# Split first loads, zero matmuls ahead of the data, and other numbers in the instruction order of a two-layer decoder trunk

## The chip, the core and the metric

The kernel runs on one core of a Trainium2 chip. The metric is the device time of one execution in microseconds (us), the median of several runs. Five engines work side by side, each through its own list of instructions in a fixed order: TensorE (PE in the profile, with its weight loads shown apart as PEld), VectorE (DVE), ScalarE (ACT), GpSimd (POOL) and SyncE (SP, which here only issues DMA transfers). An instruction whose input is not there holds up everything behind it on its engine.

## The reference

Two layers, each with one RMS norm, one wide projection and three parallel mixers; 512 tokens, 1024 features, float32 throughout. Cut to what matters:

```python
def reference(x, norm_g, w_in, ..., w_o):
    for l in range(DEPTH):                                   # DEPTH = 2
        h = rms_norm(x, norm_g[l])
        p = h @ w_in[l]                                      # 1024 -> 8776 columns
        (cb, cc, cx, cgate, q, k, v, agate, iq, ik, iw, pu, pgate, mgate) = split_columns(p)
        y_a = short_conv_mixer(cb, cc, cx, cgate, conv_w[l], w_out_conv[l])
        y_b = sparse_attention_mixer(q, k, v, agate, iq, ik, iw, ...)   # indexer, top 128 keys, softmax, 8 heads
        y_c = pool_mixer(pu, pgate, pool_w[l], pool_scale[l], w_out_pool[l])
        g = jax.nn.sigmoid(mgate.reshape(B, S, N_BRANCHES, D))
        merged = g[:, :, 0] * y_a + g[:, :, 1] * y_b + g[:, :, 2] * y_c
        x = x + merged @ w_o[l]
    return x
```

## The kernel before, in words

Everything is held transposed: features on the 128 partitions, the 512 tokens along the row. The input x is eight tiles of 128x512 (`xT[k]`), the weights are a stream of 180 chunks of 128x1024 (`wst`), 90 for each layer. Every float32 operand is split into a high part in the matmul format and the rest (`split`: ScalarE writes `hi`, VectorE subtracts and writes `lo`), and each product is three matmuls, hi by hi, hi by lo and lo by hi (`mm3`). A projection (`project`) is thus 8 slices of 3 matmuls of 128x512, 24 in all, that add up in one PSUM tile `pj`; there are four such tiles. A chunk of weights is loaded into one of two `raw` tiles and split into one of three pairs `whi` and `wlo` (`prep`); chunks are prepared three ahead (`LOOK`).

At the start the vectors `vt` (norm gains) and the x tiles are loaded, all from SyncE's queue, each x tile split with its gain (`load_x`: `xhi`, `xlo`, and a square that GpSimd adds into `ss`). The first three chunks are loaded between them, the first in four pieces, the next two in two pieces each. `wavefront` then runs three projections at once, slice by slice over k.

After that a layer runs the indexer (`select`: PE products in `sc` tiles, then 16 rounds of max and match_replace on VectorE for each of three query blocks), the pooling mixer, queries and keys (`normed`), values, the two attention passes (`attention`: scores in `sc`, transposes in `pt`, values in `pv`), the convolution mixer, three merges and the output projection.

The order written in the code is not the order that runs. The class `Order` reads all instructions with what they depend on, plays them on a model of the engines (`play`) with a duration for each (`cost`) and a delay from one engine to another (`lat`; `TO_PE` is the delay up to a matmul), and fixes the order that it finds on each engine. An engine takes, of the instructions that are ready, the one with the smallest priority; on PE the priority is the place in the code. `arrange` repeats this with new priorities (`PASSES`) and keeps the shortest. The delay from one matmul to the next that adds to the same tile is 0.003 there, so that next matmul is not yet ready at the moment PE is free, and another tile's matmul goes first.

Of the kernel before, what the change touches and what calls it, by code (L numbers as in the profile page):

```python
# [5 lines left out]
F32 = mybir.dt.float32  # L6
F32R = mybir.dt.float32r
AF = mybir.ActivationFunctionType
ALU = mybir.AluOpType
PSUM = bass.MemoryType.PSUM  # L10

LAG = 3
PASSES = 4
P = 128
S = 512
D = 1024
KT = D // P
# [12 lines left out]
class Order:  # L30
# [4 lines left out]


    LAT = {"PE": 0.2, "DVE": 0.13, "Activation": 0.14, "Pool": 0.1, "SP": 0.13}
    TO_PE = {"PE": 0.003, "DVE": 0.255, "Activation": 0.27, "Pool": 0.2, "SP": 0.27}

    def lat(self, a, b):  # L40
        return self.TO_PE[a] if b == "PE" else self.LAT[a]
# [66 lines left out]
    def cost(self, inst, kind):  # L108

        def size(a):  # L110
            n = 1
            for _, k in a.bass_ap.ap[1:]:
                n *= k
            return n

        aps = [a for a in inst.ins if hasattr(a, "bass_ap")]
        out = inst.outs[0]
        n = size(out)
        psum = any(a.bass_ap.tensor.name.split("_")[0] in ("pj", "sc", "pt", "pv") for a in aps)
        wide = [a for a in aps if size(a) > 1]  # L120
        extra = len(aps) > len(wide)
        engine = str(inst.engine).split(".")[-1]
        if kind == "InstMatmult":
            f32 = str(aps[0].dtype).endswith("float32")
            c = (0.0004167 * n + 0.003) * ((4 if n > 128 else 2) if f32 else 1)
            return c, 0.0
        if kind == "InstDMACopy":
            b = n * out.bass_ap.ap[0][1] * 4
            return (0.65 if aps[0].bass_ap.tensor.name in self.slot else 0.48), b / 360e3
        if engine == "Activation":  # L130
            return 0.093 - 0.042 * psum + 0.000833 * n + 0.093 * extra, 0.0
        if engine == "Pool":
            return (0.1 if kind == "InstMemset" else 0.1 + 0.0022 * n), 0.0
        if kind in ("InstMax", "InstMatchReplace"):
            return 0.069 + 0.00104 * max(size(a) for a in aps), 0.0
        fast = kind == "InstTensorScalarPtr" and len(wide) == 1 and not psum
        return 0.069 + 0.00104 * n * (0.5 if fast else 1) + 0.061 * extra, 0.0

# [164 lines left out]
def trunk(ctx, tc, xT, wst, vecs, cst, outT):  # L303
    nc = tc.nc
    order = Order(tc)
# [3 lines left out]
    wp = pool("wp", 3)  # L309
# [7 lines left out]
    dve, act, pe, gp = nc.vector, nc.scalar, nc.tensor, nc.gpsimd  # L317
# [11 lines left out]
    def nm(s):  # L329
        uid[0] += 1  # L330
        return f"{s}_{uid[0]}"

    def W(dt=F32, n=S):
        return wk.tile([P, n], dt, tag="w", name=nm("w"))
# [4 lines left out]
    def big(dt=F32R):  # L339
        return bp.tile([P, 4, S], dt, tag="b", name=nm("b"))  # L340
# [7 lines left out]
    def pt():  # L348
        return pp.tile([P, 4, P], F32, tag="pt", name=nm("pt"), bufs=1)
# [1 line left out]
    def pv():  # L351
        return pp.tile([P, S], F32, tag="pv", name=nm("pv"), bufs=1)

    def load(dst, src):
        nc.sync.dma_start(dst, src)  # L355


    wq = {}
# [3 lines left out]
    def prep(i):  # L362
        l, c = divmod(i, NCHUNK)
        raw = wp.tile([P, 1024], F32, tag="raw", name=nm("raw"), bufs=2)
        hi = wp.tile([P, 1024], F32R, tag="whi", name=nm("whi"), bufs=3)
        lo = wp.tile([P, 1024], F32R, tag="wlo", name=nm("wlo"), bufs=3)
        n = 1024 // (4 if i == 0 else 2 if i < 3 else 1)
        for j in range(0, 1024, n):
            p = slice(j, j + n)
            load(raw[:, p], wst[l, c, :, p])  # L370
            act.activation(hi[:, p], raw[:, p], AF.Copy)  # L371
            dve.tensor_tensor(out=lo[:, p], in0=raw[:, p], in1=hi[:, p].bitcast(F32), op=ALU.subtract)  # L372
        wq[i] = (hi, lo)

    def take():
# [11 lines left out]
    def mm(ps, lhs, rhs, start, stop):  # L387
        pe.matmul(ps, lhs, rhs, start=start, stop=stop)  # L388
# [9 lines left out]
    def split(hi, lo, src, scale=None):  # L398
        if scale is None:
            act.activation(hi, src, AF.Copy)  # L400
            dve.tensor_tensor(out=lo, in0=src, in1=hi.bitcast(F32), op=ALU.subtract)  # L401
        else:
            act.activation(hi, src, AF.Copy, scale=scale)  # L403
            dve.scalar_tensor_tensor(lo, src, scale, hi.bitcast(F32), op0=ALU.mult, op1=ALU.subtract)
# [34 lines left out]
    xs = dp.tile([KT, P, S], F32, name="xs")  # L439


    load(vt, vecs)
    for k in range(KT):
        if k in (0, 2, 4):
            prep(state["next"])
            state["next"] += 1
        if k % 4 == 0:
            xin = big(F32)
        load(xin[:, k % 4], xT[k])
        load_x(0, k, xin[:, k % 4])  # L450
    load(ct, cst)
    ob = cp.tile([P, 2, P], F32R, name="ob")
# [11 lines left out]
    def wavefront(n, src, head):  # L464

        ws = [take() for _ in range(n)]
        pss = [pj() for _ in range(n)]
        ks = [range(KT - 1), [KT - 1]]
        order = [(u, k) for k in range(KT) for u in range(n)] if head else [(u, k) for part in ks for u in range(n) for k in part]
        for u, k in order:  # L470
            c = slice(k * P, (k + 1) * P)
            mm3(pss[u], ws[u][0][:, c], ws[u][1][:, c], *src(k), k == 0, k == KT - 1)
        return pss
# [470 lines left out]
```

## Time and profile before

| | |
|---|---|
| median of 3 runs | 1079.21 us (1078.87 to 1079.73) |
| the profiled execution | 1078.84 us |
| its span, first to last instruction | 1077.1 us |
| PE busy | 1065.4 us, 4842 matmuls |
| DVE, ACT, POOL busy | 799.2, 465.5, 97.2 us |

The profile is of one execution. Its own time is 1.74 us above its span, and 0.37 us below the median of the three runs. Matmuls overlap their neighbours in the pipeline, so the busy time of PE doesn't tell how densely it works; the spacing of their starts does.

### The profile page before, as it was taken

The numbers are of one execution on the slowest core, as the hardware profiler recorded it, in microseconds if no ns is written. First come the engines' busy times: TensorE is split into PE (matmuls) and PEld (weight loads), VectorE is DVE, ScalarE is ACT, GpSimd is POOL, SyncE is SP. The second block draws the span as 40 slices with busy tenths as digits, with TensorE's granted clock in tenths as the row PEclk, the third lists the DMA queues.
The fourth block names the chain that finished last, engine by engine and source line by source line (L and its number), as shares of the span: only waits on it lengthen the run. The fifth ranks groups of instructions, "written<-read, shape, count | busy, mean of one in ns | idle before, by whom it ended". The sixth has DMA issues, their size and how long they took to land.

```text
span 1077.1 us, 13444 instructions
## 1 busy us (share of the span) xinstructions
PE 1065.4 (99%) x4842; PEld 878.4 (82%) x4842; DVE 799.2 (74%) x1389; ACT 465.5 (43%) x747; POOL 97.2 (9%) x76
## 2 busy tenths in 40 slices
PE   7999999999999999999999999999999999999998
PEld 6888888888888888888888888888888878888886
DVE  6889999997558865455559899999876598744442
ACT  6355233485233673233334542235852347623320
POOL 4000000000000011221210000000000001132210
PEclk9999999999999999999999999999999999999999
DMA  6542322452234522234535322225423245122352
GB/s 226 153 140 78 99 98 94 133 152 72 82 102 130 160 75 78 98 98 164 169 117 153 115 86 98 98 79 166 128 79 98 79 144 149 61 98 98 98 195 78
DMA packets 44402, 124.39 MB, mean 115 GB/s; under 512 B 6960, under 2 KB 7472, under 8 KB 44336
## 3 DMA queue, kind: packets, MB, share of 16 engines
q1 hardware_dynamic: 44336, 123.53, 36.4%
q8 instruction: 38, 0.62, 0.2%
q14 instruction: 28, 0.23, 0.1%
HBM read 101.49 MB, written 4.19 MB: 98 GB/s over the span
## 4 chain that ended last, share of the span: by engine, by line
PE 96%; DVE 1%; DMA 1%; issue 0%; ACT 0%; SPq 0%; DVEq 0%; ACTq 0%
PE pj L388 87%; PE sc L388 4%; PE pv L388 3%; PE pt L391 2%; DMA b<-in_x 0%; DVE wlo L372 0%; DMA k<-h 0%; DVE w L488 0%; SPq L355 0%; DVE h L401 0%; ACT whi L371 0%; DVE w L649 0%; ACT xhi L403 0%; DVE w L435 0%; DVE w L436 0%
## 5 line engine op out<-in xcount | busy, mean ns | idle before, releaser
L388 PE MATMUL pj<-xhi,whi 128*128 128x512 f32 x1040 | 373.1, 393 | 6.5 <-ACT whi L371 6.5
L388 PE MATMUL pj<-xlo,whi 128*128 128x512 f32 x1040 | 372.8, 393 | 0.0
L388 PE MATMUL pj<-xhi,wlo 128*128 128x512 f32 x1040 | 372.4, 393 | 0.0
L371 ACT ACTIVATE whi<-raw 128x1024 fp32r<-128x1024 f32 (+2 forms) x185 | 191.5, 1036 | 385.6 <-PE pj L388 358.9
L372 DVE TENSOR_TENSOR wlo<-raw,whi 128x1024 fp32r<-128x1024 f32 (+2 forms) x185 | 228.5, 1239 | 15.5 <-ACT whi L371 14.8
L388 PEld LDWEIGHTS pj<-xhi,whi 128*128 128x128 f32 x1040 | 195.0, 188 | 46.7 <-ACT whi L371 6.7
L388 PEld LDWEIGHTS pj<-xhi,wlo 128*128 128x128 f32 x1040 | 195.7, 188 | 39.4 <-DVE wlo L372 0.5
L388 PEld LDWEIGHTS pj<-xlo,whi 128*128 128x128 f32 x1040 | 195.5, 188 | 39.4
L388 PE MATMUL pj<-b,whi 128*128 128x512 f32 x640 | 210.7, 390 | 0.0
L385 DVE TENSOR_TENSOR w<-pj,ss 128x512 f32<-128x512 f32 x104 | 70.8, 684 | 93.3 <-PE pj L388 93.0
L388 PEld LDWEIGHTS pj<-b,whi 128*128 128x128 f32 x640 | 120.0, 188 | 24.2
L388 PE MATMUL pj<-b,wlo 128*128 128x512 f32 x320 | 118.2, 391 | 0.0
L610 POOL TENSOR_TENSOR b<-b,w 128x512 f32<-128x512 f32 x32 | 60.6, 1899 | 264.5 <-DVE w L608 264.4
L388 PEld LDWEIGHTS pj<-b,wlo 128*128 128x128 f32 x320 | 60.1, 188 | 12.3
L576 DVE MAX8 m<-score 128x8 f32<-128x256 f32 (+2 forms) x96 | 53.2, 557 | 1.7
L577 DVE MATCH_REPLACE8 score<-m,score 128x384 f32<-128x384 f32 (+2 forms) x96 | 52.0, 542 | 0.0
L742 DVE TENSOR_TENSOR pth<-pt,pth 128x128 fp32r<-128x128 f32 (+1 forms) x64 | 31.1, 486 | 18.7 <-PE pv L388 9.4
L819 DVE TENSOR_TENSOR w<-pj,w 128x512 f32<-128x512 f32 x16 | 11.0, 690 | 44.4 <-PE pj L388 42.8
L727 ACT ACTIVATE a<-a,mn 128x128 f32<-128x128 f32 (+1 forms) x64 | 35.6, 557 | 15.5 <-DVE mn L724 14.9
L665 POOL TENSOR_TENSOR w<-w,w 128x512 f32<-128x512 f32 x8 | 11.9, 1492 | 325.4 <-ACT w L664 325.4
L388 PE MATMUL pv<-pth,b 128*128 128x512 f32 (+3 forms) x128 | 39.9, 316 | 0.0
L741 ACT ACTIVATE pth<-pt 128x128 fp32r<-128x128 f32 (+1 forms) x64 | 27.6, 432 | 27.4 <-PE pt L391 20.1
(119 smaller groups left out, 999.7 us busy)
## 6 DMA issues: line engine op xcount, KB each, us to landing
raw<-in_w SPq DMA_DIRECT2D x177, 512.0 KB, 3.3
b<-h SPq DMA_DIRECT2D x128, 64.0 KB, 2.2
k<-h SPq DMA_DIRECT2D x64, 128.0 KB, 3.2
b<-in_x SPq DMA_DIRECT2D x8, 256.0 KB, 4.8
w<-in_x SPq DMA_DIRECT2D x8, 256.0 KB, 5.5
xs<-w SPq DMA_DIRECT2D x8, 256.0 KB, 2.3
w<-xs SPq DMA_DIRECT2D x8, 256.0 KB, 3.9
out_x<-w SPq DMA_DIRECT2D x8, 256.0 KB, 2.0
```

What stands on the lines that cost most here:

```text
L371: act.activation(hi[:, p], raw[:, p], AF.Copy)
L372: dve.tensor_tensor(out=lo[:, p], in0=raw[:, p], in1=hi[:, p].bitcast(F32), op=ALU.subtract)
L385: dve.tensor_tensor(out=out, in0=ps, in1=by, op=ALU.mult)
L388: pe.matmul(ps, lhs, rhs, start=start, stop=stop)
L391: pe.transpose(out, src, ident if n == P else ident[64:64 + n, 64:64 + n])
L576: dve.max(m8, score)
L577: dve.match_replace(score, m8, score, -3.0e38)
L610: gp.tensor_tensor(out=a, in0=a, in1=g, op=ALU.add)
L665: gp.tensor_tensor(out=s0, in0=s0, in1=s1, op=ALU.add)
L727: act.activation(pr[:, :w], pr[:, :w], AF.Exp, bias=mn, scale=-1.0, accum_out=zs)
L741: act.activation(dh, pst[:, :b + 1, :], AF.Copy)
L742: dve.tensor_tensor(out=dl, in0=pst[:, :b + 1, :], in1=dh.bitcast(F32), op=ALU.subtract)
```

## The change

Five edits. The first x tile is loaded from ScalarE's queue. The first three chunks of weights are loaded in pieces of one, one, two and four slices, each just after the x tile that its slices belong to, into two spare `b` tiles instead of `raw`, and the vectors come behind x's first tile. Six matmuls of a zeroed tile run on PE ahead of the first real one. The first wavefront takes slices 6 and 7 of a projection together. And `Order` has other numbers: no delay between two matmuls, a longer matmul, longer GpSimd operations and match_replace, and six passes instead of four.

```diff
@@ -10,7 +10,8 @@
 PSUM = bass.MemoryType.PSUM
 
 LAG = 3
-PASSES = 4
+PASSES = 6
+WARM = 6
 P = 128
 S = 512
 D = 1024
@@ -35,7 +36,7 @@
 
 
     LAT = {"PE": 0.2, "DVE": 0.13, "Activation": 0.14, "Pool": 0.1, "SP": 0.13}
-    TO_PE = {"PE": 0.003, "DVE": 0.255, "Activation": 0.27, "Pool": 0.2, "SP": 0.27}
+    TO_PE = {"PE": 0.0, "DVE": 0.255, "Activation": 0.27, "Pool": 0.2, "SP": 0.27}
 
     def lat(self, a, b):
         return self.TO_PE[a] if b == "PE" else self.LAT[a]
@@ -122,7 +123,7 @@
         engine = str(inst.engine).split(".")[-1]
         if kind == "InstMatmult":
             f32 = str(aps[0].dtype).endswith("float32")
-            c = (0.0004167 * n + 0.003) * ((4 if n > 128 else 2) if f32 else 1)
+            c = (0.000423 * n + 0.01) * ((4 if n > 128 else 2) if f32 else 1)
             return c, 0.0
         if kind == "InstDMACopy":
             b = n * out.bass_ap.ap[0][1] * 4
@@ -130,9 +131,10 @@
         if engine == "Activation":
             return 0.093 - 0.042 * psum + 0.000833 * n + 0.093 * extra, 0.0
         if engine == "Pool":
-            return (0.1 if kind == "InstMemset" else 0.1 + 0.0022 * n), 0.0
+            return (0.1 if kind == "InstMemset" else 0.1 + 0.003 * n), 0.0
         if kind in ("InstMax", "InstMatchReplace"):
-            return 0.069 + 0.00104 * max(size(a) for a in aps), 0.0
+            n = max(size(a) for a in aps)
+            return 0.069 + 0.00104 * n + 0.076 * (kind == "InstMatchReplace"), 0.0
         fast = kind == "InstTensorScalarPtr" and len(wide) == 1 and not psum
         return 0.069 + 0.00104 * n * (0.5 if fast else 1) + 0.061 * extra, 0.0
 
@@ -351,8 +353,8 @@
     def pv():
         return pp.tile([P, S], F32, tag="pv", name=nm("pv"), bufs=1)
 
-    def load(dst, src):
-        nc.sync.dma_start(dst, src)
+    def load(dst, src, queue=nc.sync):
+        queue.dma_start(dst, src)
 
 
     wq = {}
@@ -364,12 +366,8 @@
         raw = wp.tile([P, 1024], F32, tag="raw", name=nm("raw"), bufs=2)
         hi = wp.tile([P, 1024], F32R, tag="whi", name=nm("whi"), bufs=3)
         lo = wp.tile([P, 1024], F32R, tag="wlo", name=nm("wlo"), bufs=3)
-        n = 1024 // (4 if i == 0 else 2 if i < 3 else 1)
-        for j in range(0, 1024, n):
-            p = slice(j, j + n)
-            load(raw[:, p], wst[l, c, :, p])
-            act.activation(hi[:, p], raw[:, p], AF.Copy)
-            dve.tensor_tensor(out=lo[:, p], in0=raw[:, p], in1=hi[:, p].bitcast(F32), op=ALU.subtract)
+        load(raw, wst[l, c])
+        split(hi, lo, raw)
         wq[i] = (hi, lo)
 
     def take():
@@ -439,14 +437,32 @@
     xs = dp.tile([KT, P, S], F32, name="xs")
 
 
-    load(vt, vecs)
+
+    idle = W(F32R)
+    gp.memset(idle.bitcast(F32), 0.0)
+    warm = pt()
+    for n in range(WARM):
+        mm(warm.rearrange("p a b -> p (a b)"), idle[:, :P], idle, n == 0, n == WARM - 1)
+    FIRST = 3
+    raws = [big(F32).rearrange("p (a b) s -> p a (b s)", a=2) for _ in range(2)]
+    firsts = []
+    for i in range(FIRST):
+        hi = wp.tile([P, 1024], F32R, tag="whi", name=nm("whi"), bufs=3)
+        lo = wp.tile([P, 1024], F32R, tag="wlo", name=nm("wlo"), bufs=3)
+        wq[i] = (hi, lo)
+        firsts.append((raws[i // 2][:, i % 2], hi, lo))
+    state["next"] = FIRST
+    piece = {0: 1, 1: 1, 2: 2, 4: 4}
     for k in range(KT):
-        if k in (0, 2, 4):
-            prep(state["next"])
-            state["next"] += 1
         if k % 4 == 0:
             xin = big(F32)
-        load(xin[:, k % 4], xT[k])
+        load(xin[:, k % 4], xT[k], nc.scalar if k == 0 else nc.sync)
+        for i, (raw, hi, lo) in enumerate(firsts if k in piece else ()):
+            p = slice(k * P, (k + piece[k]) * P)
+            load(raw[:, p], wst[0, i, :, p])
+            split(hi[:, p], lo[:, p], raw[:, p])
+            if k == 0 and i == 0:
+                load(vt, vecs)
         load_x(0, k, xin[:, k % 4])
     load(ct, cst)
     ob = cp.tile([P, 2, P], F32R, name="ob")
@@ -466,7 +482,9 @@
         ws = [take() for _ in range(n)]
         pss = [pj() for _ in range(n)]
         ks = [range(KT - 1), [KT - 1]]
-        order = [(u, k) for k in range(KT) for u in range(n)] if head else [(u, k) for part in ks for u in range(n) for k in part]
+        if head:
+            ks = [[k] for k in range(KT - 2)] + [[KT - 2, KT - 1]]
+        order = [(u, k) for part in ks for u in range(n) for k in part]
         for u, k in order:
             c = slice(k * P, (k + 1) * P)
             mm3(pss[u], ws[u][0][:, c], ws[u][1][:, c], *src(k), k == 0, k == KT - 1)
```

What the new numbers do to the order shows best in three places. The first is PE's start. `pj_198`, `pj_199` and `pj_200` are the three projections of the wavefront, in the changed kernel `pj_218` to `pj_220`; `whi_84`/`wlo_85` is the first chunk, in the changed kernel `whi_93`/`wlo_94`. PE from its first instruction, before:

```order
L388 MATMUL pj_198<-xhi_100,whi_84 128x512
L388 MATMUL pj_198<-xlo_101,whi_84 128x512
L388 MATMUL pj_198<-xhi_100,wlo_85 128x512
L388 MATMUL pj_199<-xhi_100,whi_117 128x512
L388 MATMUL pj_198<-xhi_109,whi_84 128x512
L388 MATMUL pj_199<-xlo_101,whi_117 128x512
L388 MATMUL pj_198<-xlo_110,whi_84 128x512
L388 MATMUL pj_199<-xhi_100,wlo_118 128x512
L388 MATMUL pj_198<-xhi_109,wlo_85 128x512
L388 MATMUL pj_199<-xhi_109,whi_117 128x512
L388 MATMUL pj_198<-xhi_126,whi_84 128x512
```

and in the changed kernel:

```order
L386 MATMUL pt_84<-w_82 128x512 x6
L386 MATMUL pj_218<-xhi_111,whi_93 128x512
L386 MATMUL pj_219<-xhi_111,whi_95 128x512
L386 MATMUL pj_220<-xhi_111,whi_97 128x512
L386 MATMUL pj_218<-xlo_112,whi_93 128x512
L386 MATMUL pj_218<-xhi_111,wlo_94 128x512
L386 MATMUL pj_219<-xlo_112,whi_95 128x512
L386 MATMUL pj_219<-xhi_111,wlo_96 128x512
L386 MATMUL pj_220<-xlo_112,whi_97 128x512
L386 MATMUL pj_220<-xhi_111,wlo_98 128x512
L386 MATMUL pj_218<-xhi_129,whi_93 128x512
L386 MATMUL pj_218<-xlo_130,whi_93 128x512
```

Six matmuls of the zero tile `w_82` come first; then the three projections advance together, so that the third chunk (`whi_97`) is read by the third real matmul, where before it was first read by matmul 45.

The second place is SyncE's queue from its start (`in_x` are tiles of x, `in_v` the vectors, `in_w` pieces of weights). Before:

```order
L355 DMA b_98<-in_x 128x512
L355 DMA vt<-in_v 128x56
L355 DMA b_98<-in_x 128x512
L355 DMA raw_83<-in_w 128x256
L355 DMA raw_116<-in_w 128x512
L355 DMA b_98<-in_x 128x512
L355 DMA raw_83<-in_w 128x256
L355 DMA b_98<-in_x 128x512
```

and in the changed kernel, where ScalarE issues the first x tile:

```order
L357 DMA vt<-in_v 128x56
L357 DMA b_91<-in_w 128x128 x2
L357 DMA b_92<-in_w 128x128
L357 DMA b_99<-in_x 128x512
L357 DMA b_91<-in_w 128x128
L357 DMA b_99<-in_x 128x512
L357 DMA b_91<-in_w 128x128
L357 DMA b_92<-in_w 128x128
L357 DMA b_91<-in_w 128x256 x2
L357 DMA b_99<-in_x 128x512
```

One x tile has left the queue, and four pieces of one slice each, of all three chunks, come ahead of the third x tile, where before a quarter of the first chunk and half of the second did.

The third place is PE where the first attention pass of the first layer begins (`k_1755` and `b_1631` are keys and queries, in the changed kernel `k_1775` and `b_1651`). Before:

```order
L388 MATMUL pj_2315<-xhi_134,wlo_1915 128x512
L388 MATMUL sc_1985<-k_1755,b_1631 128x128
L388 MATMUL sc_1996<-k_1755,b_1631 128x256
L388 MATMUL sc_1985<-k_1755,b_1631 128x128
L388 MATMUL sc_1996<-k_1755,b_1631 128x256
L388 MATMUL pj_2315<-xhi_152,whi_1914 128x512
L388 MATMUL pj_2351<-xhi_109,whi_1950 128x512
L388 MATMUL pj_2315<-xlo_153,whi_1914 128x512
L388 MATMUL pj_2351<-xlo_110,whi_1950 128x512
L388 MATMUL pj_2315<-xhi_152,wlo_1915 128x512
L388 MATMUL sc_2007<-k_1755,b_1631 128x384
L388 MATMUL pj_2315<-xhi_160,whi_1914 128x512
```

and in the changed kernel:

```order
L386 MATMUL pj_1975<-xhi_196,wlo_1894 128x512
L386 MATMUL sc_2005<-k_1775,b_1651 128x128 x2
L386 MATMUL sc_2016<-k_1775,b_1651 128x256 x2
L386 MATMUL pj_2335<-xhi_111,whi_1934 128x512
L386 MATMUL pj_2335<-xlo_112,whi_1934 128x512
L386 MATMUL sc_2027<-k_1775,b_1651 128x384 x2
L386 MATMUL sc_2038<-k_1775,b_1651 128x512 x2
L386 MATMUL pj_2335<-xhi_111,wlo_1935 128x512
L386 MATMUL pj_2335<-xhi_129,whi_1934 128x512
L386 MATMUL pj_2335<-xlo_130,whi_1934 128x512
L386 MATMUL pj_2335<-xhi_129,wlo_1935 128x512
L386 MATMUL pj_2335<-xhi_146,whi_1934 128x512
```

The two matmuls of a score tile now follow each other, and so do the 24 of a projection; over the whole program a matmul writes another tile than the one ahead of it 4593 times before and 698 times in the changed kernel, and the runs of matmuls for `sc`, `pt` and `pv` between two of `pj` are 429 before and 201 now. The matmuls themselves are the same 4842 and the six of zeros.

## Rows read from the trace of the kernel before

**Rows 1.** The page: busy time of the engines, and the chain by engine.
```profile
PE 1065.4 (99%) x4842; PEld 878.4 (82%) x4842; DVE 799.2 (74%) x1389; ACT 465.5 (43%) x747; POOL 97.2 (9%) x76
...
PE 96%; DVE 1%; DMA 1%; issue 0%; ACT 0%; SPq 0%; DVEq 0%; ACTq 0%
```

**Rows 2.** The chain that ended last, 0 to 30 us: start, us, what.
```profile
1.64 3.77 DMA b<-in_x
...
5.43 0.72 ACT xhi L403
6.15 0.31 ACT whi L371
...
6.51 23.64 PE pj L388 x91
```

**Rows 3.** The same chain: its longest piece of the whole span, and its end.
```profile
409.82 154.21 PE pj L388 x680
...
1073.31 0.69 DVE w L819
```

**Rows 4.** Timeline 0 to 25 us: start, us, engine, line, operation, out<-in, count.
```profile
3.44 0.63 ACT L423 ACTIVATE a<-b 128x512 f32<-128x512 f32 x1 [1.42 <-DMA b<-in_x]
...
3.97 0.70 ACT L403 ACTIVATE xhi<-b,vt 128x512 fp32r<-128x512 f32 x1
4.13 0.61 POOL L426 COPY ss<-a 128x512 f32<-128x512 f32 x1 [3.29 <-ACT a L423]
...
6.06 0.40 ACT L371 ACTIVATE whi<-raw 128x256 fp32r<-128x256 f32 x1
...
6.88 0.62 ACT L371 ACTIVATE whi<-raw 128x512 fp32r<-128x512 f32 x1
...
7.96 1.05 PE L388 MATMUL pj<-xhi,whi 128*128 128x512 f32 x2
...
8.81 1.05 PE L388 MATMUL pj<-xlo,whi 128*128 128x512 f32 x2
...
13.99 8.37 POOL L428 TENSOR_TENSOR ss<-ss,a 128x512 f32<-128x512 f32 x5 [1.21 <-ACT a L423]
...
16.02 1.78 DVE L404 SCALAR_TENSOR_TENSOR xlo<-b,vt,xhi 128x512 fp32r<-128x512 f32 x1
...
17.73 3.47 DVE L372 TENSOR_TENSOR wlo<-raw,whi 128x512 fp32r<-128x512 f32 x2
```

**Rows 5.** Windows: PE, PEld, DVE, ACT, POOL busy, granted clock, DMA share, GB/s.
```profile
2.00:4.00 2.00, 0.00 (x0) 0.00 (x0) 0.00 (x0) 0.58 (x3) 0.00 (x0) 1.00 0.84 257
...
10.00:12.00 2.00, 2.00 (x6) 1.52 (x5) 1.98 (x4) 1.97 (x5) 0.89 (x1) 1.00 1.05 389
```

**Rows 6.** Groups of PE's instructions by line: count, busy us, mean ns.
```profile
L388 PE MATMUL pv<-pth,b 128*128 128x512 f32 (+3 forms) x128 | 39.9, 316 | 0.0
L388 PE MATMUL sc<-k,b 128*128 128x128 f32 (+3 forms) x128 | 38.8, 322 | 0.2 <-DMA k<-h 0.2
L388 PE MATMUL sc<-b,b 128*128 128x256 f32 (+2 forms) x96 | 30.1, 344 | 0.6 <-DVE w L649 0.6
L391 PE MATMUL pt<-ct,a 128*128 128x128 f32 x160 | 28.0, 273 | 0.2
```

**Rows 7.** Timeline 217.3 to 221 us, PE, first attention pass.
```profile
217.67 0.64 PE L388 MATMUL sc<-k,b 128*128 128x128 f32 x4
...
218.14 0.62 PE L388 MATMUL pj<-xhi,whi 128*128 128x512 f32 x2
...
220.09 0.39 PE L388 MATMUL pj<-xhi,wlo 128*128 128x512 f32 x1
...
220.32 0.39 PE L388 MATMUL sc<-k,b 128*128 128x512 f32 x1
```

**Rows 8.** Windows as in rows 5: ahead of, and in, layer one's attention passes.
```profile
192.00:212.00 20.00, 20.00 (x88) 16.15 (x87) 19.79 (x31) 9.81 (x14) 1.29 (x1) 1.00 0.46 130
...
217.70:269.00 51.30, 51.30 (x262) 42.53 (x262) 42.57 (x105) 35.45 (x79) 0.10 (x1) 1.00 0.36 108
361.00:412.00 51.00, 50.68 (x260) 42.05 (x259) 37.40 (x94) 38.15 (x86) 6.16 (x4) 1.00 0.34 101
```

## The prediction

> **What bounds the kernel now.** I read the busy times and the chain of waits first: PE is on 96% of the chain [rows 1], so only what PE waits for, or does slowly, can change the time. The head of the chain comes next [rows 2]: PE's first matmul starts at 6.51 us, behind the second x tile (issued at 1.64, landed at 5.41) and its split on ScalarE. The third view is a long piece of pure projections [rows 3]: 154.21 us for 680 matmuls, 0.2268 us each, and nothing else on the chain there. That spacing is PE's pace; I use it as the floor.
>
> With the floor I can say how much there is to win. The head piece has 91 matmuls in 23.64 us [rows 2]; at 0.2268 they take 20.64, so 3.0 us are lost there. The timeline shows where: at 7.96 and 8.81 us two matmuls each stand 0.425 apart [rows 4]. [...]
>
> For the rest: of the 4842 matmuls [rows 1], 128, 128, 96 and 160 are the values, scores, indexer products and transposes [rows 6], and 14 more in the order are small transposes. That leaves 4316 of 512 columns: 4316 x 0.2268 = 978.9 us. Scores and values run in widths of 128 to 512, the indexer in 256 to 512, in equal numbers, 118,784 columns together: as 232 matmuls of 512, 52.6 us. Short ones cost more than their columns: four matmuls of 128, 256, 128 and 256 columns stand between 217.67 and the next projection matmul at 218.14 [rows 7], 0.47 us for columns worth 0.34, so 0.065 extra for each of 128 columns. For the 64 of 128 columns that is 4 us, for the 174 transposes and tiny ones, at 0.057 + 0.065 = 0.12, 21 us. Sum 1056.9. PE's work runs from 6.51 to the last addition of the residual at 1073.31 [rows 3]: 1066.8. Less 1056.9 and the 3.0 of the head, some 7 us are left, over two layers, for all waits and all changes between kinds of work.
>
> So what the change can win is 6.5 us ahead of the first matmul, 3.0 of slow pace, and 7 of waits. The matmuls themselves stay.
>
> **The start.** The first x tile goes to ScalarE's queue. It was SyncE's first before and landed by 3.44 [rows 4]; I cost that at nothing. The table load that ScalarE has next waits behind the issue, and the 1.42 us in which ScalarE idles before 3.44 [rows 4] covers it. The first product needs that x tile split (starting at 3.97, 0.70 long) and one slice of `whi`. A conversion of 256 columns takes 0.40 and of 512 takes 0.62 [rows 4], so one of 128 is estimated at 0.29 on that line: 3.97 + 0.70 + 0.29 = 4.96, less the overlap of 0.1, about 4.9. The second x tile is no longer in that chain, and PE starts 1.6 us earlier.
>
> How the transfers follow is bounded by their rate. The 16 queues are 84% busy from 2 us on and full at 10 us, at 257 to 389 GB/s [rows 5]. Up to the last x tile the changed kernel moves 3.6 MB, the third chunk now among them; at about 300 GB/s that is 12 us, so the last tile lands near 14 us. PE needs it near 18. No wait there, and none if the small pieces run at half that rate for their 0.4 MB (1.3 us more).
> [...]
>
> The zeros wait for a memset of 512 columns on GpSimd. The row nearest is a copy of that size, 0.61 us [rows 4]; begun near 0.8 it ends by 1.5. Six matmuls at 0.425 take 2.6 us, so PE is free again at 4.1, before 4.9. If the memset took 1.67 us like one of the five adds (8.37 / 5 [rows 4]) they would end at 5.1, and the start would be 0.2 late. What they win lies between nothing (a gap of 0.8 us follows them, and the slow pace starts afresh) and the 3.0 us.
> [...]
>
> A new wait takes part of this back. VectorE writes every `xlo` and `wlo`; before, it ends the eight of x and eight pieces of weights at 17.73 + 3.47 = 21.2 us, at half its pace while GpSimd adds the squares (an `xlo` of 1.78 us at 16.02, beside five adds from 13.99 to 22.36 [rows 4]). Now the third chunk's pieces come ahead of the last `xlo`, which is the last of the same work. If VectorE again ends at 21.2, the last `xlo` is that late, and PE has 14 of the wavefront's 72 matmuls left: 21.2 + 3.2 = 24.4. Without that wait and at full pace it would be 4.9 + 72 x 0.2268 = 21.2; at the slow pace 3.0 more, 24.2. Before, matmul 72 ended at 6.51 + 23.64 - 19 x 0.2268 = 25.8. With another 1.0 us for x tiles that come late to VectorE the gain is 0.4, without any wait 4.6. I take 1.9: nearer to the lower end, because VectorE never rested there in the trace. In the first term nothing else moves; 12 splits instead of 8 add four instructions on two engines, some 0.3 us, inside the 1.0.
>
> **The order.** Two matmuls into one tile can follow each other. Their spacing is the floor already: from a projection's matmul at 220.09 to a score's at 220.32 the step is 0.23 [rows 7], and a projection between two tiles has the same 0.2268 [rows 3]. So neither staying in a tile nor leaving it is paid as such. Short matmuls in pairs cost what they cost alone, by the 0.065. What changes is the 7 us. If they were a price of the 429 visits to `sc`, `pt` and `pv`, the 201 left would cost 3.3 and the gain would be 3.7; if they are all waits, and the order has none, 7; if the new order waits for as much more, minus 3. The visit in rows 7 costs nothing, so I take waits, and a gain of 1.6: a chunk's tiles and PSUM tile are now in use half as long, and match_replace and GpSimd have longer durations, but a matmul that the old numbers made shorter than it is gave the other engines spare time, and that is gone.
>
> **Sum.** 1078.84 of the profiled run - 1.9 - 1.6 = 1075.3. The median lay 0.37 above that run: 1075.7. For this case alone 1072.5 to 1078.
>
> **Rivals.**
> - The start gives nothing. The zeros don't hold the pace, and VectorE's last `xlo` comes at 22: a gain of 0.5, and the order none: 1078.7. For it speaks VectorE at full load in that stretch; against it the 1.6 us of earlier start, which only this wait can eat.
> - The attention passes become VectorE's: slower. By the order PE has 39.0 and 38.3 us of matmuls from the first score to the last value of layer one's two passes, 49.0 and 44.0 before. VectorE's 105 and 94 instructions there become 93 and 92. At 42.57 / 105 = 0.405 and 37.40 / 94 = 0.398 us each [rows 8] they need 37.7 and 36.6 us, so VectorE must work 97% and 96% of a pass. If its waits for ScalarE let it reach only 90%, a pass takes 41.9 and 40.7 us, 5.3 more for a layer, 10.6 for two: 1079.2 - 1.9 + 10.6 = 1087.9. It ends slower from a share under 93%. For it: 83% and 73% in the passes now. Against: these durations overlap their neighbours, so 0.4 us is more than an instruction takes in a row of them, and ahead of the first pass VectorE works 19.79 of 20 us without a wait on PE [rows 8].
> - The visits were the price: the start wins 4.6 and the order 5: 1069.6. For it: fewer visits by half; against it the free visit in rows 7.
> - The durations don't change the waits (the change does only its first part): 1077.3; it lies inside my range and I count it with the first two.
>
> **How the numbers follow.** 0.2% is 2.2 us, about what a measurement of this kernel tells from no change: faster is below 1077.0, slower above 1081.4. My forecast has 0.55, of which 0.49 is faster; the start that gives nothing 0.22, of which 0.01 is slower and the rest the same; the slower passes 0.10, of which 0.02 stays the same; the visits 0.13, all faster. Faster 0.62, same 0.29, slower 0.09. The range reaches down half way to the visits' 1069.6 and up past 1078.7 by the uncertainty of that case: 1071.5 to 1079.9, with the far ends of the two outer cases left out.
>
> **What would show it.** Right: PE's first matmul of a projection near 4.9, after six of zeros that end near 4.1; matmul 72 ended between 22 and 25 us; projections at 0.2268 with 24 in one tile. The spacing of the first real matmuls tells whether the zeros hold the pace, an idle PE before an `xlo` whether VectorE ends the head. Wrong: PE idle in the attention passes behind VectorE or ScalarE by more than 1 us a pass, or a spacing above 0.23 within one tile.

## The result, and the profile after

The changed kernel takes 1084.75 us (median of 4 runs, 1084.32 to 1085.04), the kernel before 1079.04 (4 runs, 1078.71 to 1079.73) beside it: ratio 1.0052, 95% interval 1.0034 to 1.0069. It is 5.7 us slower; 1075.7 was forecast. The profiled execution took 1084.32 us, span 1082.5.

The page of the changed kernel, busy times and chain by engine, as [rows 1]:

```profile
PE 1072.0 (99%) x4848; PEld 876.7 (81%) x4848; DVE 801.6 (74%) x1393; ACT 459.3 (42%) x751; POOL 84.4 (8%) x77
...
PE 86%; DVE 4%; ACT 3%; DMA 2%; issue 2%; SPq 1%; POOL 0%; ACTq 0%; DVEq 0%; POOLq 0%
```

PE was 96% of the chain and is 86%: other engines now stand in it. The same by PE's waits (whom it waited for, us in total, times, longest), first of the kernel before, then of the changed one:

```profile
PE pj L388 <- ACT whi L371: 6.5, 1, 6.5
PE sc L388 <- DVE w L649: 0.6, 1, 0.6
PE sc L388 <- DVE w L401: 0.3, 1, 0.3
PE sc L388 <- DMA k<-h: 0.2, 1, 0.2
```

```profile
PE pt L386 <- POOL z L641: 1.3, 1, 1.3
PE pj L386 <- ACT whi L398: 1.0, 1, 1.0
PE pt L389 <- DVE w L547: 0.9, 2, 0.7
PE pj L386 <- DVE wlo L399: 0.8, 2, 0.4
PE pj L386 <- DVE xlo L402: 0.8, 2, 0.4
PE sc L386 <- ACT w L398: 0.6, 2, 0.3
PE sc L386 <- ACT h L398: 0.5, 1, 0.5
PE pt L389 <- DVE pth L760: 0.4, 2, 0.2
PE sc L386 <- ACT a L584: 0.3, 1, 0.3
```

Leave out the first row of each list and, in the second, the next one too (the zeros, and the gap behind them): PE stood 1.1 us before and 4.3 now. The rest hides in short waits that the modelled end of a matmul covers. So I take the starts of all matmuls from the first one of a projection on: the time from one to the next, less what it needs where nothing is waited for (0.2266 us for 512 columns, 0.170 for 384, 0.115 for 256 and for 128). A step that is shorter than that is set against the next one, and what is left is summed where it is more than 0.012. I call this sum the waits. Before it is 8.3 us, in the changed kernel 15.3, the slow pace of the head included. From that first matmul to the start of the last one, PE's time less the waits is 1058.1 us before and 1058.0 after, and 1057.5 to 1058.8 in all twenty profiles of this study. So the spacing of the new order, 24 matmuls to a tile, costs and gives nothing. Start and waits account for it all: 1.3 us earlier, 7.0 us more waits (1.66 of them up to 30 us, 3.3 at the transposes and scores of the attention passes, 2.0 elsewhere) make +5.7, against 5.48 between the two profiled executions.

**The head**, as [rows 2, 4], PE's timeline in the changed kernel (start, us, engine, line, operation, count, idle before and releaser):

```profile
1.31 2.93 PE L386 MATMUL pt<-w 128*128 128x512 f32 x6 [1.31 <-POOL z L641]
5.20 1.65 PE L386 MATMUL pj<-xhi,whi 128*128 128x512 f32 x3 [0.96 <-ACT whi L398]
...
9.64 0.63 PE L386 MATMUL pj<-xlo,whi 128*128 128x512 f32 x1
10.06 0.43 PE L386 MATMUL pj<-xhi,wlo 128*128 128x512 f32 x1
10.34 0.40 PE L386 MATMUL pj<-xhi,whi 128*128 128x512 f32 x1
...
14.13 0.50 PE L386 MATMUL pj<-xhi,wlo 128*128 128x512 f32 x1 [0.42 <-DVE wlo L399]
...
19.41 0.50 PE L386 MATMUL pj<-xlo,whi 128*128 128x512 f32 x1 [0.43 <-DVE xlo L402]
...
25.89 0.39 PE L386 MATMUL pj<-xhi,wlo 128*128 128x512 f32 x1
```

PE starts 1.3 us earlier, but works at 0.427 us a matmul up to 10.06 in spite of the zeros, and then waits for VectorE, which writes its last three `xlo` beside GpSimd's last three adds:

```profile
17.58 5.18 DVE L402 SCALAR_TENSOR_TENSOR xlo<-b,vt,xhi 128x512 fp32r<-128x512 f32 x3
...
17.45 4.75 POOL L426 TENSOR_TENSOR ss<-ss,a 128x512 f32<-128x512 f32 x3 [1.55 <-ACT a L421]
```

That is 1.73 us each, and 0.75 where VectorE is alone. Matmul 72 (the wavefront has 72) starts at 25.89 us in the changed kernel, the last row of PE above. Before, it was at 25.45:

```profile
25.45 0.39 PE L388 MATMUL pj<-xhi,whi 128*128 128x512 f32 x1
```

Nothing of the earlier start is left there.

**The attention passes**, as [rows 8]: windows from the first score to the last value of layer one's two passes (PE, PEld, DVE, ACT, POOL busy, granted clock, DMA share, GB/s), first of the kernel before, then of the changed one (there the second pass stands first):

```profile
217.70:270.70 53.00, 53.00 (x271) 44.02 (x271) 42.57 (x105) 35.65 (x80) 0.10 (x1) 1.00 0.35 105
361.40:409.60 48.20, 48.08 (x248) 40.06 (x249) 34.73 (x89) 36.11 (x83) 6.16 (x4) 1.00 0.32 94
```

```profile
358.20:401.30 43.10, 42.92 (x224) 34.31 (x222) 33.56 (x89) 34.24 (x81) 3.89 (x3) 1.00 0.35 106
215.60:259.40 43.80, 43.69 (x227) 34.91 (x225) 35.03 (x92) 34.69 (x78) 0.10 (x1) 1.00 0.34 102
```

A pass has become 9 and 5 us shorter, with as many scores and transposes in it: less of other matmuls lies between them. VectorE is busy 80% and 78% of it, ScalarE 79% each: neither is full. What PE waits for is single short steps of theirs. One such wait, in the first pass of the changed kernel:

```profile
222.15 0.39 ACT L745 ACTIVATE a<-a,mn 128x128 f32<-128x128 f32 x1
...
222.44 0.19 ACT L745 ACTIVATION_READ_ACCUMULATOR a<-a,mn 128x1 f32 x1
222.53 0.62 ACT L603 ACTIVATE w<-w 128x512 f32<-128x512 f32 x1
...
223.05 0.37 ACT L759 ACTIVATE pth<-pt 128x256 fp32r<-128x256 f32 x1
...
223.45 0.42 DVE L760 TENSOR_TENSOR pth<-pt,pth 128x256 fp32r<-128x256 f32 x1 [0.47 <-ACT pth L759]
223.51 0.40 PE L386 MATMUL sc<-k,b 128*128 128x512 f32 x1
...
224.02 0.52 PE L389 MATMUL pt<-ct,a 128*128 128x128 f32 x3
```

The transposes at 224.02 could start at 223.74, 0.227 after the score. But there is one `pt` tile, and VectorE reads the last block in it up to 223.87 (`pth`); it waited for ScalarE's copy, which stood behind an exponential, the read of its sum and a tanh of another mixer. The wait is 0.28 us. Transposes and scores have 58 such waits, 4.6 us, and had 14, 1.3 us, before.

### The profile page after: what moved, and what is told of

Its sections match the earlier page's. It is cut to its first block, busy times and chain, and to the rows that moved or that the text cites. A ratio compares the mean times of both kernels' runs of the same rounds, so it can differ in the third digit from the quotient of the medians.

```text
span 1082.5 us, 13480 instructions
## 1 busy us (share of the span) xinstructions
PE 1072.0 (99%) x4848; PEld 876.7 (81%) x4848; DVE 801.6 (74%) x1393; ACT 459.3 (42%) x751; POOL 84.4 (8%) x77
## 4 chain that ended last, share of the span: by engine, by line
PE 86%; DVE 4%; ACT 3%; DMA 2%; issue 2%; SPq 1%; POOL 0%; ACTq 0%; DVEq 0%; POOLq 0%
PE pj L386 77%; PE sc L386 4%; PE pv L386 3%; PE pt L389 2%; DMA raw<-in_w 1%; DVE wlo L399 1%; ACT whi L398 1%; DMA b<-h 1%; SPq L357 1%; ACT a L745 0%; POOL w L683 0%; DVE h L399 0%; ACT a L748 0%; DVE xlo L402 0%; ACT L745 0%
## 5 line engine op out<-in xcount | busy, mean ns | idle before, releaser
L386 PE MATMUL pj<-xhi,wlo 128*128 128x512 f32 x1040 | 408.3, 393 | 0.8 <-DVE wlo L399 0.8
L386 PE MATMUL pj<-xhi,whi 128*128 128x512 f32 x1040 | 408.0, 393 | 1.0 <-ACT whi L398 1.0
L386 PE MATMUL pj<-xlo,whi 128*128 128x512 f32 x1040 | 408.0, 392 | 0.8 <-DVE xlo L402 0.8
L398 ACT ACTIVATE whi<-raw 128x1024 fp32r<-128x1024 f32 x177 | 187.2, 1059 | 413.6 <-PE pj L386 319.1
L399 DVE TENSOR_TENSOR wlo<-raw,whi 128x1024 fp32r<-128x1024 f32 x177 | 229.3, 1297 | 30.0 <-ACT whi L398 29.6
L386 PE MATMUL pj<-b,whi 128*128 128x512 f32 x640 | 198.6, 390 | 0.0
L628 POOL TENSOR_TENSOR b<-b,w 128x512 f32<-128x512 f32 x32 | 44.8, 1399 | 280.5 <-DVE w L626 215.2
L595 DVE MATCH_REPLACE8 score<-m,score 128x256 f32<-128x256 f32 (+2 forms) x96 | 52.0, 542 | 0.0
L626 DVE SCALAR_TENSOR_TENSOR w<-w,pj 128x512 f32<-128x512 f32 x32 | 21.9, 686 | 32.2 <-ACT b L401 16.8
L398 ACT ACTIVATE h<-w 128x512 fp32r<-128x512 f32 (+1 forms) x36 | 22.7, 629 | 52.2 <-DVE w L507 22.2
```

Of the source, the lines that this page charges most:

```text
L595: dve.match_replace(score, m8, score, -3.0e38)
L626: dve.scalar_tensor_tensor(a if first else g, g, 1.0, py, op0=ALU.add, op1=ALU.mult)
L628: gp.tensor_tensor(out=a, in0=a, in1=g, op=ALU.add)
```

## The experiments

The price of an instruction is the duration that `Order` plans with. Theories: **A** (A1 in two expectations), spare time: the plan loses when its matmul is as long as the real one or longer, because every cost that it doesn't know then arrives late; **B**, the head; **C**, another order is another draw, whatever the number; **D** (A2 there), matmuls that stay in a tile cost something. They aren't longer, see above; what is left of D is that pairs leave the other engines no room in between. Times are medians; "before" is the kernel before on the same chip.

### One part of the change at a time

e1, the kernel before with all the new numbers and its own head:

```diff
+ TO_PE["PE"] 0.0; matmul 0.000423 * n + 0.01; Pool 0.1 + 0.003 * n; match_replace + 0.076; PASSES = 6
```

> The kernel before with all of the new numbers of the instruction order and six passes, its own head kept. Theory A (the new order makes PE wait in the indexer and attention stages, because matmuls are no longer priced too short and the other engines have lost their spare time): about 1084 us, the changed kernel's 1084.75 less the 0.5 that its head lost by the trace. Theory B (the head is what costs, and shifts all that follows): about 1079, as before.

Measured: 1086.44, before 1079.09, ratio 1.0069 [1.0056, 1.0081]. The numbers alone lose more than the whole change does. They also give the earlier start: with every load on SyncE's queue and no zeros, PE starts at 5.01 us in e1, since the first weights are now loaded and converted ahead of the second x tile. The second queue isn't needed for that.

e2, the changed kernel with the old numbers:

```diff
- TO_PE["PE"] 0.0; matmul 0.000423 * n + 0.01; Pool 0.1 + 0.003 * n; match_replace + 0.076; PASSES = 6
+ TO_PE["PE"] 0.003; matmul 0.0004167 * n + 0.003; Pool 0.1 + 0.0022 * n; PASSES = 4
```

> The changed kernel with the old numbers of the order and four passes. Theory A: near the kernel before, 1078.5 to 1080, since PE's lead of 1.6 us at its start is eaten by VectorE's late xlo. Theory B: near the changed kernel, 1083 or more.

Measured: 1083.34, ratio 1.0041 [1.0029, 1.0054]. That is the number that B forecast, and not A's. But it isn't lost in the head: matmul 72 starts 1.8 us earlier than before's. The new head alone gives another order for the whole program, with 10.1 us of waits outside head and attention, where before has 4.2 (C). So the losses of the numbers alone (7.4) and of the head alone (4.3) don't add up to the 5.7 of both.

e3, no delay from matmul to matmul, all else as before, and e4, the matmul's price alone (0.2266 for 512 columns in place of 0.2164):

```diff
e3
-    TO_PE = {"PE": 0.003,
+    TO_PE = {"PE": 0.0,
e4
-            c = (0.0004167 * n + 0.003) * ((4 if n > 128 else 2) if f32 else 1)
+            c = (0.000423 * n + 0.01) * ((4 if n > 128 else 2) if f32 else 1)
```

> The kernel before with one number changed: no delay between two matmuls, so that a sum goes on in its tile. Theory A1 (the matmul's longer price is the cause): 1079, the same. Theory A2 (staying in a tile is the cause: score and value matmuls that follow each other at once leave no room between): 1082 to 1084.

> The kernel before with one number changed: the matmul priced at 0.2266 us for 512 columns, as the trace has it, instead of 0.2164. Theory A1 (the short price gave every other engine 4.5% of spare time, and its loss makes PE wait): 1082 to 1084. Theory A2 (staying in a tile is the cause): 1079, the same.

Measured: 1081.89, 1.0027 [1.0016, 1.0039], and 1097.45, 1.0166 [1.0152, 1.0179]. e3 is not the 1079 of A1, and only 0.1 us under the range of A2: the delay alone costs 2.8 us in the old order, with 1.0 us more waits in attention and 3.0 more outside head and attention. That D is not the main cause of the change's loss rests on e5 below, which keeps the new delay and is 1.3 us from before. e4 speaks for A, with 18 us where 3 to 5 were forecast: the price that is right to 0.1% is the worst single edit. PE's waits in e4:

```profile
PE pj L388 <- ACT whi L371: 6.9, 2, 6.4
PE sc L388 <- ACT w L400: 4.9, 4, 1.9
PE pj L388 <- DVE z L385: 1.7, 1, 1.7
PE pj L388 <- DVE wlo L372: 1.6, 3, 0.7
```

Behind the first, the start, PE waits for all engines, in the sums of `normed` (`sc` of `w`) above all. (The prices don't add: with the other numbers in e1 the same price costs less.)

e7, six passes in the kernel before, and e8, match_replace longer there:

```diff
e7
-PASSES = 4
+PASSES = 6
e8
+            return 0.069 + 0.00104 * n + 0.076 * (kind == "InstMatchReplace"), 0.0
```

> The kernel before with six passes instead of four and no number changed: the search keeps an order that its own model plays shorter. Theory A: the spare time is the same, so 1079 or a little less. Theory C: another draw, 1081 to 1086, although the model finds it shorter.

> The kernel before with one number changed: match_replace 0.076 us longer, as the trace has it. Theory A: nearer to the chip, PE's price untouched: 1079 or less. Theory C: another draw, 1081 to 1086.

Measured: 1080.41, 1.0013 [1.0004, 1.0022], and 1083.82, 1.0048 [1.0035, 1.0061]. e7 lies between its two forecasts, e8 is C's. A truer price of match_replace loses 5 us, and neither edit touches the matmul: that is C. Each of the four single edits (e3, e4, e7, e8) made the old order worse.

### The price by steps, in the changed kernel

```diff
-            c = (0.000423 * n + 0.01) * ((4 if n > 128 else 2) if f32 else 1)
e5 +         c = (0.0004167 * n + 0.003) * ...
e6 +         c = (0.00044 * n + 0.01) * ...
e9 +         c = (0.00041 * n) * ...
e10 +        c = (0.000375 * n) * ...
e14 +        c = (0.000423 * n + 0.007) * ...
```

> The changed kernel with the matmul priced too short again (0.2164 us for 512 columns), all else as changed. Theory A (the short price gave spare time): back to 1079 to 1081, with less than 10 us of PE's waits where the changed kernel has 15. Theory C (the kernel before has one good order among many, and every change of a number draws another, mostly worse): anywhere between 1080 and 1090, no nearer to before than the changed kernel.

> The changed kernel with the matmul priced too long (0.235 us for 512 columns). Theory A: the other engines are planned with less time than they get from PE's real pace, so PE waits more: 1089 or more. Theory C: anywhere between 1080 and 1090.

> The changed kernel with the matmul priced at 0.210 us for 512 columns. Theory A (a price below PE's real pace leaves the other engines spare time): at most the 1080.2 of the 0.2164 price, some 1077 to 1080, PE's waits 7 to 10 us. Theory C (each order is a draw): 1079 to 1086.

> The changed kernel with the matmul priced at 0.192 us for 512 columns, 15% under its pace. Theory A, if spare time is all that counts: 1076 to 1079. If so short a price makes the search order the other engines for stages that PE reaches much later, it turns: 1082 or more. Theory C: 1079 to 1086.

> The changed kernel with a price of 0.2236 us for a matmul of 512 columns, between the 0.2164 of e5 (1080.16) and its own 0.2266 (1084.75). If the price acts by a dose (the shorter it is than the pace, the more spare time the other engines have in the plan), the time lies between: 1081 to 1084, and PE's waits between 10 and 15 us. If each number only draws another order, it can lie anywhere in 1079.5 to 1087, and the waits of the attention passes need not lie between.

And with the reads of sums priced, which the plan leaves out (by line, count, busy us and mean ns; the changed kernel):

```profile
L745 ACT ACTIVATION_READ_ACCUMULATOR a<-a,mn 128x1 f32 x64 | 12.1, 189 | 0.0
L742 DVE DVE_READ_ACCUMULATOR2_ANT mn<- 128x1 f32 x64 | 5.2, 81 | 0.0
```

e11 adds that price to the changed kernel, e15 has the old matmul price as well, e16 the one of e6:

```diff
+        acc = 0.09 * (len([a for a in inst.outs if hasattr(a, "bass_ap")]) > 1)
-            return 0.093 - 0.042 * psum + 0.000833 * n + 0.093 * extra, 0.0
+            return 0.093 - 0.042 * psum + 0.000833 * n + 0.093 * extra + acc, 0.0
-        return 0.069 + 0.00104 * n * (0.5 if fast else 1) + 0.061 * extra, 0.0
+        return 0.069 + 0.00104 * n * (0.5 if fast else 1) + 0.061 * extra + acc, 0.0
```

> The changed kernel with its exact matmul price, and 0.09 us added to each instruction that also sums a row (VectorE's score minimum, ScalarE's exponential), whose accumulator read the model leaves out. Theory A, with these reads as what uses up the spare time: PE's waits for transposes and scores in attention fall from 4.6 us to below 2, time 1081 to 1082.5. If the reads are not what is late: 1084 to 1086.

> The changed kernel with the 0.09 us reads of sums priced (as e11, 1080.42) and the matmul price of the kernel before, 0.2164 us (as e5, 1080.16). If both act by the spare time that the other engines get in the plan, they add up and the time is 1078.5 to 1080.0, the first that could stand with the kernel before's 1079. If one margin already gives all there is, 1080 to 1081. If the order is a draw, 1079 to 1085 without a preference.

> The changed kernel with the reads of sums priced (as e11) and a matmul price of 0.235 us, above the measured pace of 0.2266 (as e6, 1107.17). If the loss of e6 is the plan's PE being slower than the real one, so that every other engine is late for it, the reads (64 on each of two engines at 0.09 us, under 12 us in all, beside work of some 800 and 460 us) can't give that back: 1098 to 1108. If unpriced reads were the loss in e6 too, 1080 to 1090.

Measured, by price; waits from one profiled execution each ("attention": those of `pt` of `a` and `sc` of `k`; "passes": the four from first score to last value together):

| kernel | price, 512 columns | reads | median us | ratio to before, 95% | waits us | attention us (count) | passes us |
|---|---|---|---|---|---|---|---|
| before | 0.2164 | no | 1079.04 | 1 | 8.3 | 1.28 (14) | 200.8 |
| e10 | 0.192 | no | 1096.82 | 1.0164 [1.0148, 1.0180] | 25.7 | 0.16 (4) | 204.9 |
| e9 | 0.210 | no | 1080.94 | 1.0015 [1.0006, 1.0024] | 11.9 | 3.50 (18) | 185.0 |
| e5 | 0.2164 | no | 1080.16 | 1.0012 [1.0003, 1.0021] | 10.2 | 2.21 (17) | 183.1 |
| e14 | 0.2236 | no | 1084.77 | 1.0054 [1.0041, 1.0066] | 16.7 | 3.58 (37) | 178.8 |
| changed | 0.2266 | no | 1084.75 | 1.0052 [1.0034, 1.0069] | 15.3 | 4.61 (58) | 173.8 |
| e6 | 0.235 | no | 1107.17 | 1.0261 [1.0247, 1.0275] | 39.4 | 14.47 (102) | 167.7 |
| e15 | 0.2164 | yes | 1077.33 | 0.9985 [0.9976, 0.9994] | 8.1 | 0.26 (6) | 186.4 |
| e11 | 0.2266 | yes | 1080.42 | 1.0012 [1.0003, 1.0021] | 14.8 | 2.41 (22) | 173.9 |
| e16 | 0.235 | yes | 1102.22 | 1.0219 [1.0205, 1.0233] | 33.3 | 9.54 (66) | 172.9 |

(The profiled execution of e11 is its slowest, 1083.37.)

Of the forecasts by A, the times of e5, e6, e10 (there with its turn) and e16 came true. e9 was to gain on e5 and did not, e14 was to lie between e5 and the changed kernel and does not; e11 and e15 came out 0.6 and 1.2 us under their ranges, and e11's attention waits fell to 2.4 us, not below 2.

Read the table in pairs. At each of three prices the reads take off some 3 to 5 us and 2 to 5 us of attention waits. From 0.2164 up, with and without the reads, a longer price makes the passes shorter and PE's waits in them longer: the longer a matmul is in the plan, the fewer of them fill the time that it gives the other engines. That is A, with a dose. It isn't all: e14 costs as much as the changed kernel though its attention waits lie between, since 1.6 us at `pv`, 1.0 at the values' projections and 2.4 at the sums in `normed` (0.9 in the changed kernel) are its own (C). The same split shows over all orders planned without the reads. In attention, the six at 0.2164 (before, e2, e3, e5, e7, e8) wait 1.3 to 3.5 us and the three at 0.2266 (changed, e1, e4) 3.8 to 5.2: that part goes with the price. Outside head and attention the two groups overlap, 4.2 to 10.1 us and 6.2 to 17.2: there the draw hides what the price may do.

Below 0.2164 the series turns. e10 has next to no attention waits, but one long one elsewhere (timeline of VectorE and PE):

```profile
237.76 0.68 DVE L595 MATCH_REPLACE8 score<-m,score 128x512 f32<-128x512 f32 x1
238.36 0.68 DVE L383 TENSOR_TENSOR z<-pj,ss 128x512 f32<-128x512 f32 x1
...
239.18 0.77 PE L386 MATMUL pj<-xhi,whi 128*128 128x512 f32 x1 [9.09 <-DVE z L383]
```

VectorE gets to that `z`, which must free a `pj` tile, only behind the rounds of the indexer: a plan with too fast a PE thinks that there is time for them.

e15 is the first version below the kernel before, by 1.7 us. Its chain by engine, and the two passes of layer one:

```profile
PE 92%; DVE 2%; issue 2%; DMA 1%; ACT 1%; SPq 0%; DVEq 0%; ACTq 0%
```

```profile
222.70:270.50 47.80, 47.80 (x249) 39.84 (x247) 37.93 (x96) 33.35 (x77) 0.10 (x1) 1.00 0.25 84
357.90:403.50 45.60, 45.60 (x239) 38.25 (x239) 34.09 (x90) 35.69 (x83) 5.16 (x4) 1.00 0.35 103
```

PE shows no idle time in either.

### The head

e12 leaves out GpSimd's seven adds of squares in the first layer:

```diff
-        else:
+        elif l > 0:
             gp.tensor_tensor(out=xh["ss"]
```

> The changed kernel without GpSimd's seven additions of squares in the first layer (its norm is then of one slice only; 7 of 76 additions left out). If VectorE, slowed by GpSimd beside it, ends the head: xlo takes 0.7 us everywhere, PE's three waits of 1.7 us in the head are gone, matmul 72 starts at 24 us instead of 25.9. The total may move by another order downstream; the head is read from the trace.

Measured: 1081.86, 1.0028 [1.0017, 1.0038]. The last `xlo` in its timeline:

```profile
15.90 2.08 DVE L402 SCALAR_TENSOR_TENSOR xlo<-b,vt,xhi 128x512 fp32r<-128x512 f32 x3
```

0.69 us each instead of 1.73, and they end at 17.98 instead of 22.76. Every other instruction stands in the same order on its engine as in the changed kernel. The waits for `wlo` and `xlo` in the head are gone, and matmul 72 starts at 23.24, where the changed kernel has 25.89 in its first profile and 24.50 in its second (e18 below). So GpSimd's adds cost the head 1.3 to 2.7 us, by slowing VectorE. In the changed kernel each of the last three `xlo` begins inside an add and ends 0.55 us behind it, the first for instance at 19.36 beside an add from 17.45 to 18.81. In e18 the first of the three begins ahead of its add and takes 0.74 us; that is 1.0 of the 1.4 us by which its last `xlo` ends earlier.

e13 leaves out the zeros and their memset; all else stands in the same order on every engine. e17 does so to e15, and e18 is the changed kernel once more beside e17:

```diff
-    idle = W(F32R)
-    gp.memset(idle.bitcast(F32), 0.0)
-    warm = pt()
-    for n in range(WARM):
-        mm(warm.rearrange("p a b -> p (a b)"), idle[:, :P], idle, n == 0, n == WARM - 1)
```

> The changed kernel without the six multiplications of zeros and the memset ahead of them; every other instruction stands on each engine in the same order. If the zeros bring the full pace earlier, the half-rate spacing (0.427 us) after the first real matmul, near 5.2 us, lasts longer than in the changed kernel's profile (there to 10.1 us), and the time is 1 to 2 us above the changed kernel's 1084.75, so 1085.7 to 1086.8. If what the pace gives is taken back by the waits for VectorE's last pieces in the head (1.7 us in the changed kernel), matmul 72 starts within 0.4 us of the 25.9 there and the time is 1084.2 to 1085.3.

> e15 (reads of sums priced, matmul price 0.2164; 1077.33) without the zeros and their memset, every other instruction in the same order on each engine. If the zeros themselves cost the 3 us that e13 (1081.65) is below the changed kernel (1084.75), this gives 1074 to 1075.5. If the 3 us are other chips and other executions of the first loads, and the zeros do nothing, 1077 to 1078. If zeros help as meant, 1078 to 1080.

> The changed kernel as it is, beside e17 on one chip, as the counterpart of e13. If the zeros cost 3 us, it stays at 1084.3 to 1085.1, a ratio near 1.0052 to the kernel before. If e13's gain was the chip or the executions, it is at 1081 to 1083 here, a ratio near 1.0027.

Measured: e13 1081.65, 1.0027 [1.0016, 1.0038]; e17 1077.67, 0.9985 [0.9976, 0.9993], where e15 with the zeros has the same ratio; e18 1083.13, 1.0041 [1.0027, 1.0054]. e13 is below both of its forecasts, e18 between its two, e17 where the zeros do nothing. e13's lower time is not shown to be the zeros': e18's interval overlaps it, and in e17 nothing changes. None of the three shows a gain from the zeros. The timelines show why. PE's first matmuls without zeros (e13), and with them (e16):

```profile
5.21 1.65 PE L386 MATMUL pj<-xhi,whi 128*128 128x512 f32 x3 [5.21 <-ACT whi L398]
...
9.65 0.61 PE L386 MATMUL pj<-xlo,whi 128*128 128x512 f32 x1
10.07 0.42 PE L386 MATMUL pj<-xhi,wlo 128*128 128x512 f32 x1
10.33 0.40 PE L386 MATMUL pj<-xhi,whi 128*128 128x512 f32 x1
```

```profile
1.31 2.93 PE L387 MATMUL pt<-w 128*128 128x512 f32 x6 [1.31 <-POOL z L642]
5.15 0.96 PE L387 MATMUL pj<-xhi,whi 128*128 128x512 f32 x3 [0.91 <-ACT whi L399]
5.95 0.39 PE L387 MATMUL pj<-xlo,whi 128*128 128x512 f32 x1
6.18 0.40 PE L387 MATMUL pj<-xhi,wlo 128*128 128x512 f32 x1
```

e13's slow pace ends at 10.07, where the changed kernel's ends, with no zeros at all. In e16, e2 and e5, with the same six zeros and the same gap, PE has the full pace from the second real matmul on; in the nine other profiles with zeros it has not, up to 9 to 11 us. What set the pace stays open. And the pace isn't what ends the head: in twelve of the thirteen profiles with the new head and GpSimd's adds, zeros or not, half pace or full, matmul 72 starts 3.1 to 3.2 us behind the end of the last `xlo`, which comes at 21.2 to 23.7 us (the thirteenth is e2, with 2.5 us and the old numbers). A faster PE only waits longer for VectorE there.

## Why the prediction was wrong

- **The floor** was right: 0.2266 us in both orders, and PE's work without waits the same to 0.1 us. "Neither staying in a tile nor leaving it is paid" held, and so no gain came from the 228 visits saved.
- **The start**: 4.9 forecast, 5.20 came (the wait ends with `whi`); 1.3 us of the 1.6. Most of the 0.3 is the first x tile, whose move to ScalarE's queue was costed at nothing: ScalarE first reads it at 3.61 to 3.76 us in the fourteen profiles with that queue, at 3.42 to 3.57 in the six without. The memset took 0.53 us and ended at 1.26, the zeros at 4.24, near the 1.5 and 4.1 of the text. What the zeros win was left between nothing and the 3.0 us of slow pace there; in the runs the gap behind them was followed by half pace in nine profiles and by full pace in three, and what sets the pace is not shown.
- **The head's term, -1.9**, failed in size. VectorE was the new wait, as named, but with `wlo` too. The path was right: matmul 72 follows the last `xlo` by the 14 matmuls that were counted. But that `xlo` ended at 22.76, not 21.2. Start and head together gave +0.35 in the changed kernel's profile (1.31 earlier, 1.66 more waits), and -0.96 in e18's (1.27 earlier, 0.31 more). The rival "the start gives nothing" told this part.
- **The order's term, -1.6**, is the step that made the forecast wrong. It read: "I take waits, and a gain of 1.6", with "a matmul that the old numbers made shorter than it is gave the other engines spare time, and that is gone" as one of its reasons. The prediction set it against the gain, but far too small: it outweighs the other reasons, and so the term has the other sign. The waits outside the head went from 5.51 to 10.86 us, +5.35 (11.28 in e18). The term's lower bound, 3 us more, was too near. With the old price (e5) 4.6 us come back, with the reads priced (e11) 4.3, with both (e15) 7.4 (by the first median; the second, in e18, is 1.6 lower). The prediction looked for waits in the old order that a better table would remove; there were only 5.5, and a truer price of one engine in a table where others are too short takes cover away.
- **VectorE as the bound of the passes**: the right stage, the wrong mechanism. 97% and 96% were forecast from 39.0 and 38.3 us of matmuls a pass. That counts columns alone, without the extra that the prediction itself gives to short matmuls; passes took 43.8 and 43.1, and 42.6 and 41.9 without their waits. VectorE was 80% and 78% busy, and PE lost 3.3 us in all four instead of 10.6. The sign named for "wrong", over 1 us a pass, is what came: 4.61 / 4.
- **Not weighed at all**: that a new order is a draw. e3, e7, e8 and e2 moved the time by +1.6 to +5.0 us without a longer price of the matmul. How much of the 5.35 us is such scatter isn't settled. Of its parts, the 3.3 us of the attention passes go with the price: 2.4 of them come back with the old price (e5), 2.2 with the reads priced (e11). The 2.0 us elsewhere lie within the scatter.

## What to carry over

Where a planner's durations fix the order, the price of the engine that bounds should leave room for what the table doesn't know of the others. So make the missing steps (here the reads of sums) known before that price is made exact. In this kernel a price a few per cent short did best: 0.2164 with the reads priced, for a pace of 0.2266, is the lowest of ten (1077.33); at 0.192 the time was 17 us longer than before. A new table is a new order: judge it by several tables around it, not by one. An earlier start of PE was worth only what the slowest chain into the same stage, here VectorE's, allowed.

## What the runs showed of the hardware

- Six matmuls of zeros and a gap of about 1 us were followed by half pace (0.427 us for 512 columns) in nine of twelve profiles and by full pace (0.227) in three. The granted-clock column reads 1.00 in both, so the spacing has to be read.
- VectorE's `xlo` of 512 columns took 0.69 to 0.75 us alone (the last three of e12, and the changed kernel's at 6.81 us). The changed kernel's last three took 1.73 us each (5.18 in all); each began inside an add of GpSimd (three in 4.75 us) and ended 0.55 us behind it.
- The read of a sum is an instruction of its own, 0.19 us busy on ScalarE and 0.08 on VectorE, and putting 0.09 us for each of the 64 of either into the plan took 2.8 to 5.0 us off the whole.
